# Order of work at six places in a one-core MLA and spatial-gating layer

## The chip, the cores and the metric

The kernel runs on one core of one Trainium2 chip. A core has five engines that run side by side: TensorE (PE in the profile; PEld are its weight loads), VectorE (DVE), ScalarE (ACT), GpSimd (POOL) and SyncE (SP), which here only issues DMAs. Each engine takes its instructions in the order in which the program gives them, and each instruction waits for the semaphores of what it needs. The metric is the device time of one execution in microseconds (us); lower is better.

## The reference

One decoder layer for 512 tokens of width 2048, all in float32. The input is normed and modulated by a conditioning vector c, and one wide projection gives all branches. Cut to what matters here:

```python
mod = c_act @ w_ada[l] + b_ada[l]
shift, scale, gate = jnp.split(mod, 3, axis=-1)
h = rmsnorm(x, attn_norm_g[l]) * (1.0 + scale[:, None]) + shift[:, None]
proj = h @ w_in[l]
q_lat, kv_lat, k_rope, z_mla, u, v, z_sgu, g_mla, g_sgu = split_cols(proj, IN_SPLITS)
q = (rmsnorm(q_lat, q_norm_g[l]) @ w_uq[l])...      # 16 heads, 128 plain and 64 rotary columns
kv = (rmsnorm(kv_lat, kv_norm_g[l]) @ w_ukv[l])...  # 16 heads, 128 key and 128 value columns
y_mla = causal_mla_attention(q_nope, q_rope, k_nope, k_rope, v_mla) * jax.nn.silu(z_mla)
y_sgu = chunked_causal_sgu(u, v, sgu_norm_g[l], w_spatial[l], b_spatial[l]) * jax.nn.silu(z_sgu)
merged = jax.nn.sigmoid(g_mla) * y_mla + jax.nn.sigmoid(g_sgu) * y_sgu
x = x + gate[:, None] * (merged @ w_out[l])
```

At the end stands a final norm. The spatial gate mixes v over the 128 tokens of a chunk with a lower triangular matrix for each of 16 groups.

## The kernel before

**Products in three matmuls.** To keep float32 accuracy, each operand is split in a high part (a cast to fp32r, on ACT) and a low part (the difference, on DVE), and a product is three matmuls: high by high, high by low, low by high. `mm3` (L147 to L150) issues them for ordinary products, L1384 to L1386 for the big projection. So each tile of weights that comes from DRAM costs an ACT cast and a DVE subtraction before TensorE can use it. The parts live in a few buffers that are used in turn (`w0h`/`w0l`, `w1h`/`w1l` and, in the projection, a third pair under the name X).

**The projection in blocks.** After the first products (L443 and the loops behind it) come 11 blocks of 28 granules. A granule is one slot of the order of work: 12 matmuls of 512 columns. The products of two column blocks are built from seven sums, so DVE also adds weights before it splits them (`v_sum`, `v_t3`), and POOL issues DMAs that add to what is in the buffer (`v_add`).

**The order inside a slot.** What happens beside the matmuls is entered by `on(slot, phase, f, ...)` (L703). In each slot the phases run in the order of L701, all but the last two ahead of the slot's matmuls, and inside a phase in the order of registration:

```python
FIRST, HIGH, EVAC, GATE, SPLIT, BACK, MISC, LOAD = range(8)
```

The cast of a granule's weights (`v_split`) stands in HIGH and its low part (`v_low`) in SPLIT, both two slots ahead of the granule's matmuls (two granules of a block have them in SPLIT and MISC). These are registered first, for all blocks at once (L741 to L765). Copies out of PSUM stand in EVAC, DMA issues in LOAD. All work of second rank stands in BACK: a small planner, `place` (L713), adds up DVE's cost by slot, moves an item on to the first slot with room, and enters it there in BACK.

**Work of second rank that the change touches.**
- *Shares* (L1008 to L1026, L1140): 52 partial sums of the shift vector with the columns of the first weights. Each share loads 256 KB by SP (`share_load`, LOAD phase, three buffers: `half0`, `half1`, `cosT`) and adds on DVE (`share`, BACK). The load of share i is entered in the slot in which share i-3 is done, and the first three loads all in one slot, three after the rotary tables' last step. Share i is placed at least four slots behind its load.
- *Mix* (L930 to L946, L971 to L996): for each of 16 groups `sgu_gain` scales v, `sgu_split` splits it (`sinT` high on ACT, `vl` low on DVE), and `sgu_mix`, in the next slot's MISC, is the three matmuls of the mixing product. `t_gate` (L952) is a gate product of 128x1024 on DVE that is placed in the same way.
- *Latent splits at the seam* (L1309, L1334 to L1348): in the last slots of the projection (-7 to -1) the ten tiles of the normed latents are split for the attention (`lat_split`, two ACT casts and two DVE subtractions for each pair), next to the three steps of the key's rotation (`key_rotary`, L1271) and the splits of the first attention weights (`ws.split_to`, L103). Slot 0 is where the attention's products begin: `rproj` (the rotary queries), `qproj`, `kproj`, `vproj`.

**The heads** (L1667 to L1719). For each head h: the scores, the softmax (masks, maxima and scaling on DVE, exponentials on ACT), in the meantime the next head's query product `qproj(h + 1)`, then ten 128x128 transposes of the probabilities in three groups (`transposes`, L1594), the next head's key product `kproj(h + 1)`, and the product with v. From head 12 on (`GATED`) the probabilities are scaled on DVE ahead of the transposes. Weights come through a stream (`Stream`, L68): `get` splits the weights of the next product ahead of their use and issues the DMAs of those behind. `bank()` gives the PSUM banks in turn; a bank is free when the copy of its last product out of it is done. The v product of a pair of heads is taken out of two banks by `finish` (L1538), which waits in the list `merging` until the next query product.

**Output gate dots** (L1434 to L1455, L54): the first half of the output gate needs 32 partial dots on DVE (`piece_sum`, 0.6 us each), spread over the heads by the table `PIECES`. The dots of an odd head stand inside its softmax, those of an even head behind its product with v; head 15's stand behind its transposes, right ahead of the sum that ends them.

Of the kernel before, what the change touches and what calls it, by code (L numbers as in the profile page):

```python
# [25 lines left out]
H = 16  # L26
# [24 lines left out]

SHIFT_AT = (17, 18, 19, 20, 20, 21, 22, 24, 25, 26, 27, 29, 31, 33, 35, 37)
NG = 8
PIECES = (2,) * 13 + (0, 3, 3)  # L54

INV_FREQ = np.array([
    0x3f800000, 0x3f3ff911, 0x3f0ff59a, 0x3ed7e89b, 0x3ea1e89b, 0x3e72d423, 0x3e361887, 0x3e088d77,
# [71 lines left out]
def trunk_layer(ctx, tc, xT, xn, c, vecs, pos, wada, w1, w2, wv, wv3, wv4, wh, wh15, wq, wqr, wk, wvv, wo, wsT, bsp, gfin, out,  # L129
# [53 lines left out]
    ws = Stream(nc, [(wp, f"wraw{i}") for i in range(3)], [(wp, f"w{i}") for i in range(2)])  # L183
# [83 lines left out]
    gq, gr, gk, gvv = {}, {}, {}, {}  # L267
# [45 lines left out]
    def get(i, ahead=1, run=1):  # L313
        r = ws.get(i, ahead)
        fs, pend[:] = pend[:run], pend[run:]
        for f in fs:
            f()
        return r
# [11 lines left out]
    def bank():  # L330
        n_bank[0] += 1
        return bank_at(ring[(n_bank[0] - 1) % len(ring)])
# [89 lines left out]
    for j in range(KC):  # L422
# [4 lines left out]
        wH, wL = get(g1[j], ahead=0)  # L427
# [76 lines left out]
    for j in range(KC):  # L504
        fix_begin(j)
        wH, wL = get(g2[j])
# [136 lines left out]
    for st in range(KC):  # L643
# [5 lines left out]
        wH, wL = get(gb[st], ahead=0 if st == KC - 1 else 1)  # L649
# [51 lines left out]
    FIRST, HIGH, EVAC, GATE, SPLIT, BACK, MISC, LOAD = range(8)  # L701

    def on(s, phase, f, *a):  # L703
        assert s >= done[0], (s, done)
        events.setdefault(s, {}).setdefault(phase, []).append(lambda: f(*a))
# [4 lines left out]
    def spend(s, us):  # L710
        busy[s] = busy.get(s, 0.0) + us

    def place(s, us, f, *a):  # L713

        def full(s):
            own, (a, b) = busy.get(s, 0.0) + us, (busy.get(s + d, 0.0) for d in (-1, 1))
            near = [sum(busy.get(s + d + k, 0.0) for k in range(5)) for d in range(-4, 1)]
            return own > 3.3 or own + max(a, b) > 5.75 or s < at_block[T0] + 22 and max(near) + us > 13.4

        while full(s):  # L720
            s += 1
        spend(s, us)
        on(s, BACK, f, *a)
        return s

    def run(s, *phases):
# [140 lines left out]
    for b in range(1, len(BLOCKS)):  # L867
# [11 lines left out]
        for key in (bl, br_, al, ar):  # L879
            if key[0] == "v":  # L880
                for t in range(2):
                    n, o = 2 * key[2] + t, key[1] * S
# [87 lines left out]
    for g in range(H):  # L970
        c, q = divmod(g, 4)  # L971
        on(s_, MISC, v_load, g)
        on(s_, LOAD, gain_load, g)
        a = s_ + 4
        on(a, BACK, sgu_scale)
        a = place(a, 0.29, sgu_weights)
        a = place(a, 0.29, sgu_weights_split)
        if g + 1 < H:
            on(a + 1, LOAD, sgu_load, g + 1)
        a = place(max(a, s_ + 5), 0.69, sgu_gain)  # L980
        a = place(a + 1, 0.69, sgu_split)
        s_ = max(a + 1, out_at[g - 2], max(ready["u", c, half] for half in range(2)) - 2)
        on(s_, MISC, sgu_mix, g)
        for half in range(2):
            out_at[g] = place(max(s_ + 1, ready["u", c, half] + 1), 0.46, sgu_out, g, half)
            last_out[g, half] = out_at[g]
        if q == 3:
            for half in range(2):
                stored[c, half] = max(last_out[k, half] for k in range(4 * c, g + 1)) + 1
                stored[c, half] = max(stored[c, half], gated[c, half] + 1)  # L990
                on(stored[c, half], LOAD, t_store, c, half)
# [141 lines left out]
    rope_end = rope_make(at_block[1] + 6)  # L1133
# [3 lines left out]
        on(s, MISC, shift_turn, 4 * q)  # L1137
        return place(s + 1, 0.6, shift_sum, 4 * q)

    used, biased = [rope_end + 3] * 3, []  # L1140
    s_ = used[0]
    for i, (q, ks, _) in enumerate(shares):
        on(used[-3], LOAD, share_load, i)
# [71 lines left out]
    for group in (((10, "lat8"), (11, "lat9")), ((12, "lat10"), ("plain", "sinT"))):  # L1215
# [9 lines left out]
        i = group[0][0]  # L1225
# [108 lines left out]
    on(s_att, LOAD, to_attention)  # L1334
    for i in range(10):
        on(s_att + (0, 0, 2, 2, 4, 4, 5, 5, 6, 6)[i], LOAD, lat_fetch, i)
        if i < 8:
            on((-7, -7, -5, -5, -3, -3, -2, -2)[i], BACK, lat_split, i)

    def first_weights(n):  # L1340
        ws.limit = gr[0] + n
# [2 lines left out]
    for n, s_ in enumerate((-7, -5, -3, -1)):  # L1344
        on(s_, LOAD, first_weights, n)
    on(-1, HIGH, lambda: ws.split_to(gr[0]))
    on(-1, MISC, lambda: ws.split_to(gq[0]))
    ws.next_raw, ws.next_part = 0, 1  # L1348

# [2 lines left out]
    for b in range(len(BLOCKS)):  # L1352
        if b == 1:
            ring[:], n_bank[0] = [5, 6], 0
        for g, (p, i) in enumerate(V7):
            s = done[0] = at_block[b] + g
            n = 1 if b or g else 2
# [15 lines left out]
            if i == 0 and p in (1, 5, 6):  # L1373
                which, banks = {1: ("y", y_of[b % 2]), 6: ("z", z_of), 5: ("w", z_of if b else (5, 6))}[p]
                v7[which] = [bank_at(k) for k in banks]
            ps = v7["y" if p < 5 else "z" if p > 5 else "w"]
            wH, wL = (w.rearrange("p (k h w) -> p k h w" if BLOCKS[b][0] == "v" else "p (h k w) -> p k h w", h=4, k=2)
                      for w in vparts.pop((b, g)))
# [20 lines left out]
    place = {}  # L1399
# [13 lines left out]

    krh, krl = at("krh", F32R), at("krl", F32R)
    hilo(krh, krl, kr[0])
    for i in (8, 9):
        lat_split(i)
    for key, at_ in ready.items():
        if at_ >= 0:
# [30 lines left out]
    def pieces_at(h):  # L1450
        k = sum(PIECES[:h])
        for i in range(k, k + PIECES[h]):
            piece_sum(i)
# [21 lines left out]
        load_before(gk[h], fetch, h)  # L1475


    qt, kt, vv, qs = {}, {}, {}, {}

    def qproj(h, meanwhile=None, then=None):  # L1480
        wH, wL = get(gq[h])
# [28 lines left out]
        tt(b[lo_], r[hi_], b[hi_].bitcast(F32), ALU.subtract)  # L1510
        qs[2 * p], qs[2 * p + 1] = a, b

    def kproj(h):
        wH, wL = get(gk[h])
        ps = bank()
        for k in range(4):
            sl = slice(k * P, (k + 1) * P)
            mm3(ps, wH[:, sl], wL[:, sl], lh[6 + k], ll[6 + k], k == 0, k == 3)
        return ps
# [28 lines left out]
    def scores(h):  # L1548
        qh, ql = qt.pop(h)
        kh, kl = kt.pop(h)  # L1550
        q2 = qs.pop(h)
        s3, s2, s1 = bank(), bank(), bank()
        dst = {3: s3, 2: s2[:, :384], 1: s1[:, :256], 0: s1[:, 256:384]}
        for i in (3, 2, 1, 0):
            ps = dst[i]
            n = (i + 1) * P
            q = slice(i * P, (i + 1) * P)
            mm3(ps, qh[:, q], ql[:, q], kh[:, :n], kl[:, :n], True, False)

            PE.matmul(ps, q2[:, q], krh[:, :n], start=False, stop=False)  # L1560
            PE.matmul(ps, q2[:, q], krl[:, :n], start=False, stop=True)  # L1561
        return dst
# [31 lines left out]
    def transposes(pr_, js):  # L1594
        w = sum((NB - j) * P for j in js)
        ps = bank()[:, :w]
        o = 0
        for j in js:
            for i in range(j, NB):
                PE.transpose(ps[:, o:o + P], pr_[i][:, j * P:(j + 1) * P], ident)  # L1600
                o += P
        th = at(f"th{js[0]}", F32R)[:, :w]
        tl = at(f"tl{js[0]}", F32R)[:, :w]
        parts = {}
        o = 0
        for j in js:
            n = (NB - j) * P
            parts[j] = (th[:, o:o + n], tl[:, o:o + n])
            o += n
        return parts, lambda: hilo(th, tl, ps)  # L1610
# [41 lines left out]
    ps = kproj(0)  # L1652
# [5 lines left out]
    def out_granule(cg, i, banks, ahead=1, run=1):  # L1658
        wH, wL = get(go[cg, i], ahead, run)
        for k in range(2):  # L1660
            j = 2 * i + k
            sl = slice(k * 512, (k + 1) * 512)
            for n in range(NB):
                tk = slice(n * P, (n + 1) * P)
                mm3(banks[n], mh[j][:, tk], ml[j][:, tk], wH[:, sl], wL[:, sl], j == 0, j == H - 1)

    for h in range(H):  # L1667
        if h == H - 1:
            ring[:], n_bank[0] = [4, 5, 6, 7], 0
            ws.split_to(go[0, 0])  # L1670
        dst = scores(h)
        more, odd = h + 1 < H, h % 2 == 1
        pair = h // 2 + 1
        first = go[0, 1] if not more else gr[pair] if not odd and 2 * pair < H else None
        pr_, shares_ = softmax(h, dst, (lambda: ws.split_to(first)) if first is not None else None)
        if more:
            qproj(h + 1, lambda: merge(1 if h == H - 2 else None))
            if not odd and 2 * pair < H:
                rps = rproj(pair)
        else:  # L1680
            pso = [bank_at(k) for k in range(NB)]
            for i in range(2):
                out_granule(0, i, pso)
        pa, fa = transposes(pr_, (0,))
        fa()
        if h < GATED:
            for n in range(NB):
                g_ = gt[h][:, n * P:(n + 1) * P]
                ACT.activation(g_, g_, AF.Copy, scale=shares_[:, n:n + 1])
        pb, fb = transposes(pr_, (1,))  # L1690
        fb()
        pc, fc = transposes(pr_, (2, 3))
        fc()
        if more:
            kps = kproj(h + 1)
            kfinish(h + 1, kps)
        else:
            merge()
            pieces_at(h)
            DVE.tensor_reduce(out=dots[:, 2 * KC:2 * KC + NG], in_=partial, axis=AX.X, op=ALU.add)  # L1700
            gate_sum(0, NG)
            out_granule(0, 2, pso)
            gate_turn(0, NG, bank(), nt(tp, [P, S], F32, "sig", bufs=3))()
        gate_ = gt[h]
        if h < GATED:
            gate_ = nt(tp, [P, S], F32, "sig", bufs=3)
            ACT.copy(gate_, turn(gt[h]))
        tps = turn(vt[h])
        ops = pv(h, {**pa, **pb, **pc})
        merge_a(h, ops, tps, gate_)  # L1710
        if not odd:
            pieces_at(h)
        if not odd and 2 * pair < H:
            m2 = at("m2", F32)
            swapped(m2, rps)
        if more and odd:
            rfinish(pair, rps, m2)
            vproj(pair)
# [192 lines left out]
```

## Time and profile before

| what | us |
|---|---|
| median of 3 runs (range) | 1564.72 (1563.97 to 1565.47) |
| the profiled execution | 1566.76 |
| its span, first to last instruction | 1565.1 |
| TensorE matmul busy | 1552.7 |
| VectorE busy | 1218.7 |
| ScalarE busy | 802.9 |
| GpSimd busy | 70.5 |

The profile is of one execution. A row of a timeline shows the start in us, the duration, the engine, the line of the kernel, the operation, the tiles (out<-in), the shape and the count; in brackets stands the idle time of the engine just before it and what ended it. Matmuls overlap, so the ends of their rows are modelled and a stall is read from the difference of two starts. A row of the chain of waits shows start, duration and name. A row of DMA issues shows the tiles, the queue, the count, the size and the us from issue to landing. `ps` are PSUM banks, `d` and `lat` are tiles of the latents' area that several things share, `hh`/`hl` high and low parts of the activations.

### The profile page before, as it was taken

The page shows a single profiled execution, that of the slowest core. Times are in us where ns is not written, and L with a number is a line of the kernel's source. Part 1 is how long each engine was busy: PE and PEld are TensorE (multiplying, and loading weights), DVE is VectorE, ACT ScalarE, POOL GpSimd, SP SyncE. Part 2 cuts the span into 40 slices and gives each one's busy share as a digit, 9 for nine tenths or more (in the row PEclk, how much of TensorE's full clock was granted, in tenths as well). Part 3 has the DMA queues.
Part 4 walks back from the last instruction along what each step waited for, and adds up shares of the span by engine and source line. Part 5 has one row for each costly group of instructions (what it writes and reads, how often), then busy time and mean ns, then how long its engine had stood idle before and what let it go on. Part 6 is the DMA issues. An engine that isn't in the chain of part 4 may idle for free.

```text
span 1565.1 us, 20574 instructions
## 1 busy us (share of the span) xinstructions
PE 1552.7 (99%) x7392; PEld 1296.2 (83%) x7392; DVE 1218.7 (78%) x1667; ACT 802.9 (51%) x1238; POOL 70.5 (5%) x67
## 2 busy tenths in 40 slices
PE   9999999999999999999999999999999999999998
PEld 7888778888888888888888888888888888888887
DVE  8989777778787879787879797878777777865753
ACT  4445555546545555545555565647655555532332
POOL 0000000101010101020100010100000000000000
PEclk9999999999999999999999999999999999999999
DMA  9979565858785877786867685967443433348722
GB/s 377 376 273 353 163 190 162 240 138 243 231 234 171 233 216 214 210 227 192 224 183 204 203 253 160 258 164 223 142 122 122 127 112 118 96 133 333 262 88 108
DMA packets 237224, 316.16 MB, mean 202 GB/s; under 512 B 16201, under 2 KB 184193, under 8 KB 231489
## 3 DMA queue, kind: packets, MB, share of 16 engines
q1 hardware_dynamic: 214210, 291.78, 57.0%
q0 software_dynamic: 22912, 23.07, 9.6%
q8 instruction: 58, 0.95, 0.2%
q14 instruction: 44, 0.36, 0.1%
HBM read 291.11 MB, written 23.68 MB: 201 GB/s over the span
## 4 chain that ended last, share of the span: by engine, by line
PE 91%; DMA 3%; DVE 3%; ACT 1%; issue 1%; SPq 0%; DVEq 0%; ACTq 0%
PE ps L1384 16%; PE ps L1386 16%; PE ps L1385 16%; PE ps L149 12%; PE ps L150 12%; PE ps L148 12%; PE ps L443 5%; DMA X<-in_wh 2%; PE ps L1600 1%; PE ps L1626 1%; DMA wraw<-in_w 1%; PE ps L1560 1%; PE ps L1561 1%; DVE X L136 1%; DVE d L136 0%
## 5 line engine op out<-in xcount | busy, mean ns | idle before, releaser
L136 DVE TENSOR_TENSOR X<-X,X 128x1024 fp32r<-128x1024 f32 (+2 forms) x111 | 130.5, 1182 | 32.7 <-ACT X L629 31.1
L629 ACT CAST X<-X 128x1024 fp32r<-128x1024 f32 x70 | 73.6, 1052 | 100.0 <-PE ps L1385 54.4
L629 ACT CAST w0h<-X 128x1024 fp32r<-128x1024 f32 x70 | 73.7, 1052 | 97.7 <-PE ps L1385 54.3
L629 ACT CAST w1h<-X 128x1024 fp32r<-128x1024 f32 x69 | 72.6, 1052 | 79.3 <-PE ps L1385 43.7
L136 DVE TENSOR_TENSOR w0l<-X,w0h 128x1024 fp32r<-128x1024 f32 x70 | 85.5, 1221 | 28.1 <-ACT w0h L629 27.9
L136 DVE TENSOR_TENSOR w1l<-X,w1h 128x1024 fp32r<-128x1024 f32 x69 | 84.3, 1221 | 24.7 <-ACT w1h L629 23.6
L119 DVE TENSOR_TENSOR w0l<-wraw,w0h 128x1024 fp32r<-128x1024 f32 (+4 forms) x61 | 64.3, 1053 | 40.4 <-ACT w0h L118 37.9
L118 ACT CAST w0h<-wraw 128x1024 fp32r<-128x1024 f32 (+4 forms) x61 | 56.0, 918 | 75.2 <-PE ps L150 21.1
L118 ACT CAST w1h<-wraw 128x1024 fp32r<-128x1024 f32 (+4 forms) x60 | 50.5, 841 | 83.7 <-PE ps L150 21.9
L136 DVE TENSOR_TENSOR X<-wraw,X 128x1024 f32<-128x1024 f32 (+1 forms) x65 | 79.3, 1221 | 17.2 <-ACT X L629 15.0
L1386 PE MATMUL ps<-w1l,hh 128*128 128x512 f32 x236 | 91.9, 390 | 0.2 <-DVE w1l L136 0.2
L1384 PE MATMUL ps<-w1h,hh 128*128 128x512 f32 x236 | 91.9, 389 | 0.0
L1385 PE MATMUL ps<-w1h,hl 128*128 128x512 f32 x236 | 91.9, 389 | 0.0
L1385 PE MATMUL ps<-w0h,hl 128*128 128x512 f32 x236 | 91.8, 389 | 0.0
L1384 PE MATMUL ps<-w0h,hh 128*128 128x512 f32 x236 | 91.8, 389 | 0.0
L1386 PE MATMUL ps<-w0l,hh 128*128 128x512 f32 x236 | 91.8, 389 | 0.0
L1386 PE MATMUL ps<-X,hh 128*128 128x512 f32 x232 | 90.6, 391 | 0.2 <-DVE X L136 0.2
L1384 PE MATMUL ps<-X,hh 128*128 128x512 f32 x232 | 90.4, 390 | 0.0
L1385 PE MATMUL ps<-X,hl 128*128 128x512 f32 x232 | 90.3, 389 | 0.0
L139 DVE SCALAR_TENSOR_TENSOR wada<-wada,cact 128x2048 f32<-128x2048 f32 x39 | 88.9, 2282 | 0.6 <-DMA wada<-in_wada 0.6
L119 DVE TENSOR_TENSOR w1l<-wraw,w1h 128x1024 fp32r<-128x1024 f32 (+4 forms) x60 | 57.4, 957 | 33.6 <-ACT w1h L118 32.7
L148 PE MATMUL ps<-hh,w1h 128*128 128x512 f32 x204 | 81.3, 399 | 0.0
(410 smaller groups left out, 4418.3 us busy)
## 6 DMA issues: line engine op xcount, KB each, us to landing
X<-in_wh SPq DMA_DIRECT2D x131, 512.0 KB, 5.0
wada<-in_wada SPq DMA_DIRECT2D x39, 1024.0 KB, 7.4
wraw<-in_wo SPq DMA_DIRECT2D x32, 512.0 KB, 4.2
wraw<-in_wh SPq DMA_DIRECT2D x21, 512.0 KB, 4.7
wraw<-in_wh POOLq DMA_DIRECT2D x21, 512.0 KB, 7.9
X<-in_wv SPq DMA_DIRECT2D x17, 512.0 KB, 3.7
X<-in_wh SPq DMA_DIRECT2D x22, 384.0 KB, 5.2
wraw<-in_w SPq DMA_DIRECT2D x16, 512.0 KB, 9.5
```

Of the source, the lines that this page charges most:

```text
L118: self.nc.scalar.copy(hi[:, :n], raw[:, :n])
L119: self.nc.vector.tensor_tensor(out=lo[:, :n], in0=raw[:, :n], in1=hi[:, :n].bitcast(F32), op=ALU.subtract)
L136: DVE.tensor_tensor(out=out, in0=in0, in1=in1, op=op)
L139: DVE.scalar_tensor_tensor(out=out, in0=in0, scalar=scalar, in1=in1, op0=op0, op1=op1, **kw)
L148: PE.matmul(ps, ah, bh, start=start, stop=False)
L149: PE.matmul(ps, ah, bl, start=False, stop=False)
L150: PE.matmul(ps, al, bh, start=False, stop=stop)
L443: PE.matmul(ps1[m], a[:, cols[m]], b, start=(j == 0 and a is wH and b is hh[j]), stop=False)
L629: ACT.copy(hi, t)
L1384: PE.matmul(ps[t].rearrange("p (h w) -> p h w", h=4), xh[:, tk], wH[:, k], start=st, stop=False, skip_group_check=True)
L1385: PE.matmul(ps[t].rearrange("p (h w) -> p h w", h=4), xl[:, tk], wH[:, k], start=False, stop=False, skip_group_check=True)
L1386: PE.matmul(ps[t].rearrange("p (h w) -> p h w", h=4), xh[:, tk], wL[:, k], start=False, stop=sp, skip_group_check=True)
```

## The change

It moves work at six places; nothing is computed in another way.

1. `PIECES`: head 12 gives up its two dots, heads 14 and 15 change from 3 and 3 to 2 and 4, head 15's four go ahead of its transposes, and two come last, where head 15's stood.
2. `sgu_split` is entered in the SPLIT phase in place of BACK, in the slot that the planner gives it as before.
3. The first three share loads are entered in three slots, one each, in place of one.
4. Of the latent splits, numbers 2 and 3 (slot -5) go from BACK to SPLIT.
5. Latent splits 6 and 7 go from slot -2, BACK, to slot -1, HIGH, behind the split of the first rotary query weights.
6. At head 14 the key product of head 15 is cut in two: its weights are split ahead of head 14's scores, its first half (six matmuls) runs ahead of head 14's transposes, the second half stays where the whole was. The PSUM bank of this product is so taken ahead of those of the transposes.

```diff
-PIECES = (2,) * 13 + (0, 3, 3)
+PIECES = (2,) * 12 + (0, 0, 2, 4, 2)
...
-    def place(s, us, f, *a):
+    def place(s, us, f, *a, phase=BACK):
...
-        on(s, BACK, f, *a)
+        on(s, phase, f, *a)
...
-        a = place(a + 1, 0.69, sgu_split)
+        a = place(a + 1, 0.69, sgu_split, phase=SPLIT)
...
-    used, biased = [rope_end + 3] * 3, []
+    used, biased = [rope_end + 3 + n for n in range(3)], []
...
-        if i < 8:
-            on((-7, -7, -5, -5, -3, -3, -2, -2)[i], BACK, lat_split, i)
+        if i < 6:
+            on((-7, -7, -5, -5, -3, -3)[i], SPLIT if i in (2, 3) else BACK, lat_split, i)
...
     on(-1, HIGH, lambda: ws.split_to(gr[0]))
+    for i in (6, 7):
+        on(-1, HIGH, lat_split, i)
...
-    def kproj(h):
-        wH, wL = get(gk[h])
-        ps = bank()
-        for k in range(4):
+    def kproj(h, ks=range(4)):
+        if ks[0] == 0:
+            kw[h] = (*get(gk[h], 1 if len(ks) == 4 else 0), bank())
+        else:
+            ws.split_to(gk[h] + 1)
+        wH, wL, ps = kw[h]
+        for k in ks:
...
+        if h == H - 2:
+            ws.split_to(gk[h + 1])
         dst = scores(h)
...
             for i in range(2):
                 out_granule(0, i, pso)
+            pieces_at(h)
+        halved = h == H - 2
+        if halved:
+            kproj(h + 1, range(2))
         pa, fa = transposes(pr_, (0,))
...
-            kps = kproj(h + 1)
+            kps = kproj(h + 1, range(2, 4) if halved else range(4))
...
             merge()
-            pieces_at(h)
+            pieces_at(H)
```

More of the change, by code (lines that the diff above doesn't have):

```diff
@@ L1415, in trunk_layer @@
     hilo(krh, krl, kr[0])
-    for i in (8, 9):
+    for i in range(8, 10):
         lat_split(i)
@@ L1475, in trunk_layer @@
         load_before(gk[h], fetch, h)
-    qt, kt, vv, qs = {}, {}, {}, {}
+    qt, kt, vv, qs, kw = {}, {}, {}, {}, {}
     def qproj(h, meanwhile=None, then=None):
```

## The prediction

> **What bounds the kernel now.** I read the page first, for the engine that sets the end, then the PE timeline for the places where it stands still, then for each such place the timeline of the engine that releases it, and the chain of waits for the one place that a transfer decides.
>
> ```profile
> span 1565.1 us, 20574 instructions
> PE 1552.7 (99%) x7392; PEld 1296.2 (83%) x7392; DVE 1218.7 (78%) x1667; ACT 802.9 (51%) x1238; POOL 70.5 (5%) x67
> ```
>
> TensorE is busy for 1552.7 of 1565.1 us, so an order of work can only win back short stalls. A stall is measured best from start to start. A 512-column matmul starts 0.23 us after the one ahead of it; what a step takes beyond that is lost. The edits speak to five groups of such steps. I take them one by one, and ask each time what is late next.
>
> **Share loads.** The stall is the step 394.11 to 394.90:
>
> ```profile
> 394.11 0.39 PE L1386 MATMUL ps<-w1l,s 128*128 128x512 f32 x1
> 394.90 0.50 PE L1384 MATMUL ps<-w0h,s 128*128 128x512 f32 x1 [0.40 <-ACT d L842]
> 395.24 0.39 PE L1385 MATMUL ps<-w0h,s 128*128 128x512 f32 x1
> ```
>
> 0.79 - 0.23 = 0.56 us, and the next step takes 0.34 instead of 0.23, another 0.11, which I add after every stall. Together 0.67. The chain of waits says why: a PSUM copy on ACT stands behind a cast that waits for one weight load.
>
> ```profile
> 381.37 11.85 DMA X<-in_wh
> 379.96 0.33 SPq L1014 DMA_DIRECT2D half<-in_w  x1
> 380.82 0.49 SPq L1014 DMA_DIRECT2D cosT<-in_w  x1
> 383.03 0.56 SPq L884 DMA_DIRECT2D v_d<-d  x1
> half<-in_w SPq DMA_DIRECT2D x1, 256.0 KB, 6.1
> v_d<-d SPq DMA_DIRECT2D x1, 256.0 KB, 12.4
> 389.07 0.75 DVE L139 SCALAR_TENSOR_TENSOR rx<-half,shift,rx 128x512 f32<-128x512 f32 x1
> 390.00 1.23 DVE L136 TENSOR_TENSOR w0l<-X,w0h 128x1024 fp32r<-128x1024 f32 x1 [0.18 <-ACT w0h L629]
> ```
>
> SP issues the three share loads (256 KB each, from 379.96), then this weight load (512 KB, at 381.37), then two stores of v. The edit leaves share 0 where it is and puts the weight load and both stores ahead of shares 1 and 2. Share 0 lands at 379.96 + 6.1 = 386.1 and the second store at 383.03 + 12.4 = 395.4. Between them land share 1, share 2, the weight load and two stores: 1536 KB in 9.3 us, 165 KB per us. If the queue keeps its order and its pace, the weight load now lands at 386.1 + 512/165 = 389.2, well ahead of its 393.2, and the 0.67 goes.
>
> What is late next: share 1, now behind 512 + 512 KB, lands at 386.1 + 1280/165 = 393.9. The planner still gives it its old slot, and DVE comes to it at 389.07. Behind it in DVE's order stands the w0l of row 390.00, which the third matmul of the group at 394.90 reads. Without a stall that matmul starts at 394.11 + 3 x 0.23 = 394.8. Now w0l ends 1.94 us after share 1 has landed (0.05, 0.75 less 0.09 overlap, 1.23), at 395.8: a new stall of 1.0 + 0.1. **Net +0.5.** Bounds: no stall if share 1 lands by 392.8 (net -0.7); landing last of the group, at 395.4, it costs 2.6 + 0.1 (net +2.0). I take the middle, since order and bytes are known and only the pace is assumed.
>
> The Trainium skill, page "DMA: Bandwidth & Descriptors", section "Rules for kernel authors", tells authors to issue a transfer early and wait for it late. By that rule moving share 1 back can only hurt; by the row of the 11.85 us it also frees the weight load, and my sum keeps both.
>
> **Mix's v split.** The edit moves the two halves of the split (ACT, then DVE) from the BACK phase of their slot to the SPLIT phase. There the low part of the weights was registered earlier and still comes first, so only what stands in BACK ahead of the split is passed. By the order of registration that is a gate product in 2 of the 16 slots, and nothing in the other 14.
>
> ```profile
> 777.01 1.22 DVE L136 TENSOR_TENSOR d<-d,d 128x1024 f32<-128x1024 f32 x1
> 778.14 0.68 DVE L136 TENSOR_TENSOR vl<-lat,sinT 128x512 fp32r<-128x512 f32 x1
> 778.27 0.39 PE L148 MATMUL ps<-sinT,whl 128*128 128x512 f32 x1
> 778.88 0.50 PE L149 MATMUL ps<-vl,whl 128*128 128x512 f32 x1 [0.22 <-DVE vl L136]
> 542.42 0.39 PE L148 MATMUL ps<-sinT,whl 128*128 128x512 f32 x1
> 542.73 0.50 PE L149 MATMUL ps<-vl,whl 128*128 128x512 f32 x1
> ```
>
> With vl ahead of the 1.22 us product it is ready 1.1 us earlier, more than the 0.61 - 0.23 = 0.38 that PE waits; at 542 the wait is 0.08. With 0.11 behind each: **-0.7**. The product is late by 0.6 instead, and only its store to DRAM waits for that. The other mix stalls of this stage stay. Bounds: -0.7 and 0.
>
> **Latent splits at the seam.** Here are two stalls, 1072.11 to 1072.66 and 1078.05 to 1078.67:
>
> ```profile
> 1065.63 2.51 ACT L1285 COPY d<-rx 32x512 f32<-32x512 f32 x4
> 1068.92 1.41 DVE L139 SCALAR_TENSOR_TENSOR hl<-b,vec,hh 128x512 fp32r<-128x512 f32 x2 [0.43 <-ACT hh L1313]
> 1071.39 1.22 DVE L136 TENSOR_TENSOR w1l<-wraw,w1h 128x1024 fp32r<-128x1024 f32 x1
> 1072.11 0.39 PE L1385 MATMUL ps<-w1h,hl 128*128 128x512 f32 x1
> 1072.66 0.50 PE L1386 MATMUL ps<-w1l,hh 128*128 128x512 f32 x1 [0.16 <-DVE w1l L136]
> 1077.80 0.83 ACT L118 CAST w0h<-wraw 128x768 fp32r<-128x768 f32 x1 [1.89 <-PE ps L1385]
> 1078.05 0.39 PE L149 MATMUL ps<-hl,w1h 128*128 128x512 f32 x1
> 1078.67 0.50 PE L150 MATMUL ps<-hh,w1l 128*128 128x512 f32 x1 [0.23 <-DVE w1l L119]
> 1088.09 1.22 DVE L119 TENSOR_TENSOR w0l<-wraw,w0h 128x1024 fp32r<-128x1024 f32 x1
> 1089.36 0.39 PE L149 MATMUL ps<-w0l,hh 128*128 128x256 f32 x1
> ```
>
> Splits 2 and 3 go ahead of the four copies of the key's rotation, so DVE no longer idles 0.43 for them. Its w1l ends 0.43 earlier and the first stall of 0.32 + 0.11 goes: **-0.4**. Splits 6 and 7 go behind the split of the first query weights, whose w1l then needs 1.4 us less of DVE ahead of it; ACT's two casts fit into its idle 1.89. So the second stall, 0.39 + 0.11, goes too. But it is **given back**: vproj's second matmul at 1089.36 starts as w0l ends (1088.09 + 1.22 = 1089.31), with no room. That w0l hangs on a run of ACT and DVE work that begins with the cast at 1077.80, which waits for the matmuls ahead of the second stall and not for those behind it. PE comes 0.5 earlier to a w0l that does not. I count 0 for it; the bounds are 0 and -0.5.
>
> **Output gate dots and the half key product.**
>
> ```profile
> 1341.66 0.68 DVE L139 SCALAR_TENSOR_TENSOR piece<-piece,cq 128x512 f32<-128x512 f32 x1
> 1347.25 0.39 PE L150 MATMUL ps<-hh,w0l 128*128 128x512 f32 x1
> 1348.21 0.44 PE L1600 MATMUL ps<-ident,hl 128*128 128x128 f32 x2 [0.58 <-DVE hl L143]
> 1349.28 0.47 PE L148 MATMUL ps<-hh,w1h 128*128 128x512 f32 x1
> 1366.85 0.68 DVE L119 TENSOR_TENSOR w0l<-wraw,w0h 128x512 fp32r<-128x512 f32 x1
> 1367.55 0.38 PE L1600 MATMUL ps<-ident,hl 128*128 128x128 f32 x2
> 1369.16 0.48 PE L148 MATMUL ps<-hh,w0h 128*128 128x512 f32 x1
> 1383.02 0.39 PE L148 MATMUL ps<-w0h,b 128*128 128x512 f32 x1
> 1383.33 0.50 PE L149 MATMUL ps<-w0l,b 128*128 128x512 f32 x1
> 1389.94 1.16 DVE L136 TENSOR_TENSOR hl<-ps,hh 128x512 fp32r<-128x512 f32 x2 [4.37 <-ACT hh L153]
> ```
>
> Head 13's transposes wait for its softmax: 0.96 - 0.23 = 0.73. Head 12's two dots (about 0.61 each) stand on DVE ahead of that softmax and leave: 1.2 against 0.73, **-0.73**. Head 14's ten transposes take 1369.16 - 1367.55 = 1.61 where head 13's take 1.07: **-0.54** is lost between them, on PSUM banks that the v product's split frees behind the w0l of 1366.85. The change moves that split ahead of the scores and puts six matmuls, 1.4 us, ahead of the transposes. The moved split may delay the softmax by up to its 0.68; the 1.4 covers it (without that cover it would cost the 0.68). The bank now taken first is one that was freed second, by a split that also comes 0.68 earlier. Head 14's third dot leaves, 0.6, which ends the 0.08 + 0.11 at 1383.33: **-0.2**. Four dots come into head 15's wait, 2.5 us inside the idle 4.37 of row 1389.94; without that cover they would delay the transposes' low parts, not the transposes. One load of output weights is issued later, still ahead of the whole first granule that comes before its use. Sum -1.5; bounds -1.5 and -0.7 (if the head 14 edits fail).
>
> **The sum.** -1.5 - 0.7 - 0.4 + 0.5 = -2.1 us. The profiled execution took 1566.76 (its span and 1.66 around it), so such a one would take 1564.7. The median of the runs is 1564.72, 2.0 lower; taking its stalls to be the same, it gives 1562.6.
>
> **The rivals.**
> (1) Share 1 lands in time. For: the idle of DVE ahead of 394 and a pace that differs between groups. Against: the same engines carry the same bytes. Time: -2.6 - 0.67 = -3.3, 1561.4. The Trainium skill, "DMA: Bandwidth & Descriptors", section "Anatomy of one DMA", has a fixed 2 us plus bytes over 436 GB/s, an estimated 2.6 us for 256 KB; by that share 1 would land long before 389 and this rival would hold. The trace's 6.1 us for share 0 speaks against it.
> (2) More is given back than at vproj. The head stalls come back where the next softmax step is as late; only 0.4 of the 1.5 and half of the mix stay: -0.3 - 0.4 - 0.4 + 0.5 = -0.6, 1564.1. Against: each released engine there waits for PE itself.
> (3) Slower: a late share holds SP too. The load of share 4 uses share 1's buffer, so SP cannot issue it, nor what stands behind it, until share 1 is done. If lateness passes from share 1 to 4, 7, 10 and on at 1.1 us each, the change turns slower with the second of these (-2.1 + 2 x 1.1 = 0.1), and five of them give +3.4, 1568.1. Against: the queue is backlogged there, so a later issue need not land later.
>
> **How the numbers follow.** Forecast 0.50, rival 1 0.22, rival 2 0.21, rival 3 0.07. A measurement of this kernel tells about 0.2%, 3.1 us, from no change. Faster by more than that is most of rival 1 and little else: 0.18. Slower is rival 3, less its milder half: 0.05. Within: 0.77. The range runs from all gains kept (-2.6 - 0.67 - 0.5 = -3.8, 1560.9) to share 1 landing last of its group (-0.6, 1564.1) with the scatter of the runs, 0.5: 1564.6.
>
> **What would show it.** Right: no long step at 394.1, but one on the third matmul behind it, with a DVE wait for a share's load; 778 and 542 in step; the seam's first stall gone and a new wait of about 0.5 at vproj's second matmul; even steps at heads 13 and 14. Wrong: a share wait that ends by 392.8, a mix that still waits for vl at 778, or scores that come late in head 14.

## The result and the profile after

| | before | after |
|---|---|---|
| median of 22 runs (range), us | 1565.48 (1563.97 to 1566.70) | 1563.18 (1562.49 to 1565.24) |
| ratio of the runs, 95% interval | | 0.9986 (0.9980 to 0.9992) |
| the profiled execution | 1566.76 | 1565.08 |

The change makes the kernel 2.2 us faster by the ratio, 2.3 by the medians. The forecast was a change of -2.1 and 1562.6. The interval excludes no change; the size, 0.14%, is below the 0.2% from which the forecast spoke of faster. The head of the page of the changed kernel:

```profile
span 1563.4 us, 20578 instructions
PE 1551.1 (99%) x7392; PEld 1297.3 (83%) x7392; DVE 1219.0 (78%) x1667; ACT 802.7 (51%) x1238; POOL 70.2 (4%) x67
```

The work of each engine is as before; only TensorE's waits differ. Now the places of the prediction, one by one, on the timelines of the changed kernel.

**Share loads.** TensorE first, then DVE:

```profile
394.08 0.39 PE L1387 MATMUL ps<-w0h,s 128*128 128x512 f32 x1
395.94 0.50 PE L1388 MATMUL ps<-w0l,s 128*128 128x512 f32 x1 [1.47 <-DVE w0l L136]
```

```profile
387.49 1.23 DVE L136 TENSOR_TENSOR w1l<-wraw,w1h 128x1024 fp32r<-128x1024 f32 x1 [0.77 <-ACT w1h L629]
394.00 0.75 DVE L139 SCALAR_TENSOR_TENSOR rx<-half,shift,rx 128x512 f32<-128x512 f32 x1 [5.28 <-DMA half<-in_w]
394.67 1.22 DVE L136 TENSOR_TENSOR w0l<-X,w0h 128x1024 fp32r<-128x1024 f32 x1
```

The old stall is gone and the foreseen new one is there: DVE stands 5.28 us at share 1, w0l waits behind it, and the third matmul of the group comes 1.86 - 0.23 = 1.63 us late. The landing at 394.0 is what the prediction had (393.9). The stall is larger than its 1.0, because TensorE was 0.5 us further on when it came there.

**A place not foreseen,** near 776:

```profile
776.02 0.39 PE L1387 MATMUL ps<-X,hl 128*128 128x512 f32 x1
776.83 0.50 PE L1388 MATMUL ps<-X,hh 128*128 128x512 f32 x1 [0.43 <-DVE X L136]
```

0.81 - 0.23 = 0.58 us are lost here for the low part of a product that no edit touches.

**Heads.** Head 13's transposes follow the product ahead of them after 0.23, where it was 0.96. Head 14's ten take 1369.08 - 1368.07 = 1.01, where it was 1.61:

```profile
1347.19 0.39 PE L150 MATMUL ps<-hh,w0l 128*128 128x512 f32 x1
1347.42 0.38 PE L1605 MATMUL ps<-ident,hl 128*128 128x128 f32 x2
...
1368.07 0.38 PE L1605 MATMUL ps<-ident,hl 128*128 128x128 f32 x2
...
1369.08 0.47 PE L148 MATMUL ps<-hh,w0h 128*128 128x512 f32 x1
```

These two traces leave a question. The waits at 395.94 and 776.83 cost 1.74 and 0.69 us with the 0.11 behind each, and yet the change is as fast as forecast with a smaller loss. And the profiled execution of before, 1566.76, was slower than all 22 timed runs (up to 1566.70). How many of the stalls on which the prediction rests belong to the kernel, and how many to the one execution that was profiled?

### The profile page after: what moved, and what is told of

The parts are those of the page before. It is cut to its first block, busy times and chain, and to the rows that moved or that the text cites. A ratio compares the mean times of both kernels' runs of the same rounds, so it can differ in the third digit from the quotient of the medians.

```text
span 1563.4 us, 20578 instructions
## 1 busy us (share of the span) xinstructions
PE 1551.1 (99%) x7392; PEld 1297.3 (83%) x7392; DVE 1219.0 (78%) x1667; ACT 802.7 (51%) x1238; POOL 70.2 (4%) x67
## 4 chain that ended last, share of the span: by engine, by line
PE 50%; DVE 1%; issue 0%; ACT 0%; DVEq 0%
PE ps L149 9%; PE ps L150 9%; PE ps L148 9%; PE ps L1388 6%; PE ps L1386 6%; PE ps L1387 6%; PE ps L1605 1%; PE ps L1631 1%; PE ps L1565 1%; PE ps L1566 1%; DVE d L136 0%; PE ps L1187 0%; PE ps L1177 0%; DVE X L136 0%; DVE w0l L119 0%
```

## The experiments

All times are medians in us (range); "before" is the kernel before, measured beside it on the same chip.

| kernel | runs | time | before | ratio (95%) |
|---|---|---|---|---|
| share loads alone | 11 | 1565.35 (1565.02 to 1566.17) | 1565.22 | 1.0000 (0.9991 to 1.0009) |
| share loads, share 1 a slot later | 11 | 1565.27 (1565.09 to 1565.58) | 1565.22 | 0.9999 (0.9991 to 1.0008) |
| mix alone | 11 | 1564.75 (1564.37 to 1565.07) | 1565.22 | 0.9995 (0.9987 to 1.0004) |
| heads alone | 11 | 1563.88 (1563.22 to 1564.78) | 1565.22 | 0.9991 (0.9982 to 0.9999) |
| before, again | 1 | 1565.13 | 1565.59 | |
| changed kernel, again | 1 | 1562.91 | 1565.59 | |
| seam alone | 11 | 1565.49 (1565.33 to 1566.37) | 1565.59 | 1.0000 (0.9991 to 1.0009) |
| seam and activations later | 11 | 1564.57 (1564.22 to 1565.33) | 1565.59 | 0.9994 (0.9985 to 1.0002) |
| dots' table alone | 11 | 1564.57 (1564.00 to 1564.78) | 1565.32 | 0.9994 (0.9985 to 1.0002) |
| all but the share loads | 11 | 1563.18 (1562.74 to 1565.02) | 1565.32 | 0.9987 (0.9979 to 0.9996) |
| the same, activations later | 11 | 1562.17 (1561.92 to 1563.34) | 1565.32 | 0.9981 (0.9972 to 0.9989) |
| all, share 1 and activations later | 11 | 1562.06 (1561.75 to 1562.45) | 1565.32 | 0.9979 (0.9970 to 0.9988) |

The intervals reach about 1.4 us to each side, so single edits are told apart by the traces. The experiments ran on three chips; the medians of before on them and in the first measurement (1565.48) lie within 0.4 us, which speaks against the chip as the reason for a long execution. All these kernels issue the same number of matmuls, so the start of matmul number k can be set side by side. The next table counts it from matmul 120 (at 18.6 us, behind the loads of the start), subtracts the second profile of before (below, "Both kernels once more"), and takes the difference from column to column; the headings give the stretch by the time of before. Negative is gained. The last column is the whole.

```
                        to 400  546    781    1093   1353   1372   end  | whole
before, first profile     1.01  0.05   0.14   0.35   0.05   0.01   0.04 |  1.65
changed, first profile    1.80 -0.21   0.23  -0.15  -0.71  -0.61  -0.18 |  0.17
changed, again            0.00 -0.21  -0.35  -0.11  -0.76  -0.61  -0.20 | -2.24
share loads alone         0.50  0.00   0.15  -0.16   0.06   0.02   0.05 |  0.62
share 1 a slot later      0.01  0.00   0.15  -0.02   0.03   0.02   0.03 |  0.22
mix alone                 0.01 -0.21  -0.41  -0.12   0.07   0.02   0.05 | -0.59
heads alone               0.00 -0.01   0.27  -0.12  -0.71  -0.61  -0.20 | -1.38
seam alone                0.31  0.01   0.11  -0.11   0.07   0.00   0.00 |  0.39
seam, activations later   0.04  0.18   0.45  -0.82  -0.12   0.03   0.05 | -0.19
dots' table alone         0.04  0.00   0.07  -0.09  -0.74   0.01  -0.21 | -0.92
all but share loads       0.01 -0.21  -0.17  -0.15  -0.71  -0.61  -0.18 | -2.02
same, activations later  -0.01 -0.22  -0.32  -0.76  -0.94  -0.62  -0.20 | -3.07
all, share 1, act. later  0.00 -0.22  -0.01  -0.80  -0.96  -0.60  -0.21 | -2.80
```

### The share loads alone, and with share 1 a slot later

The first kernel has this edit alone, the second this and the next:

```diff
-    used, biased = [rope_end + 3] * 3, []
+    used, biased = [rope_end + 3 + n for n in range(3)], []
```
```diff
-        s_ = place(max(used[-3] + 4, s_ + 1), 0.75 if len(ks) == 1 else 1.4, share, i)
+        s_ = place(max(used[-3] + (5 if i == 1 else 4), s_ + 1), 0.75 if len(ks) == 1 else 1.4, share, i)
```

> The kernel before with the share loads' edit alone. My working: the 0.67 us lost at 394.90 go, share 1 lands near 394 us, and the third matmul of its group starts when the low part w0l behind the share ends, at about 395.8; net +0.5 us against before. The trace of the changed kernel has this wait at 1.63 + 0.11 us (start 395.94), because TensorE reached the place about 0.5 us earlier there; if the start is set by the landing alone, it is again near 395.9 here, however early TensorE comes, and the net against before stays at +0.4 to +0.6. Rival 1 (share 1 lands in time): no step above 0.5 us there, -0.7. Rival 3 (lateness passes on to later shares): further DVE waits for share 4, 7, 10, more than +2. Also to be seen here: if a new wait near 776.8 us (0.59 in the changed kernel, not foreseen) appears in this kernel, it comes with the loads and not with the mix edit.

> The share loads' edit alone, and share 1 is allowed one slot later on DVE, so that the low part w0l stands ahead of it. Theory: the loss is only that DVE stands at share 1 with w0l queued behind; the loads' new order by itself is a gain. Then the steps at 394 to 396 are even, and the kernel is 0.67 us faster than before and 1.1 us faster than with the edit alone; DVE still idles for share 1 until about 394, with nothing urgent behind it. Rival: the wait moves to the next product (X low part) or to later shares, which now run a slot late through their buffers: between 0 and +0.5 against before.

Measured: 0.13 and 0.05 us slower in the medians, nothing within their intervals. The edit alone loses 0.50 by 400 us in its profile. Its timeline of TensorE, and that of DVE:

```profile
394.18 0.39 PE L1385 MATMUL ps<-w0h,s 128*128 128x512 f32 x1
394.71 0.50 PE L1386 MATMUL ps<-w0l,s 128*128 128x512 f32 x1
```

```profile
392.77 0.75 DVE L139 SCALAR_TENSOR_TENSOR rx<-half,shift,rx 128x512 f32<-128x512 f32 x1 [4.10 <-DMA half<-in_w]
393.44 1.22 DVE L136 TENSOR_TENSOR w0l<-X,w0h 128x1024 fp32r<-128x1024 f32 x1
```

The mechanism is that of the prediction (DVE idle at share 1, w0l behind it), but share 1 lands at 392.77, not 394.0, and the stall is 0.30. So my "start again near 395.9" fell: the landing moves from execution to execution. With share 1 a slot later the steps are even, as the theory said, but the 0.67 us that should then be won against before aren't there. The comparison was with a stall that the runs of before don't have: in the stretch to 400 this kernel and the second profile of before agree within 0.01.

### The mix alone, and the heads alone

The mix kernel passes `phase=SPLIT` in the one call for `sgu_split`; the heads' kernel has the table and the two halves of the key product, as in the change.

> The kernel before with the mix's v split in the SPLIT phase alone. My working: -0.7 us, the steps at 778.88 and 542.73 become even, all other steps stay. The changed kernel has a wait of 0.59 us at 776.83 for the low part of another product. If the mix edit makes it, it is here too, and the net is about -0.1. If it comes from where the weight load of 748 us landed (0.9 us later in that trace, ahead of any moved instruction), it is absent here, or present by chance only, and the net is -0.7.

> The kernel before with the output gate dots' table and the half key product alone. My working: -1.5 us: head 13's transposes no longer wait (0.73), head 14's ten transposes run through (0.54), the step at 1383.33 is even (0.2). Rival 2 (given back at the next softmax step): the same stalls gone but a new one behind them, -0.4 in all.

Measured: -0.47 and -1.34 in the medians. By the stretches the mix gains 0.21 at 542 and 0.41 up to 781; the heads 0.71 and 0.61 and 0.20. No wait is passed on behind them: the columns to their right are as in the kernels without these edits. Both leave the share loads alone, and in both profiles the stall of 394.90 is missing. That spoke for chance in the first profile, and the next two runs were for this.

### Both kernels once more

> The kernel before once more, unchanged, for a second profiled execution of it. In two kernels that leave the share loads as they were (the mix edit alone, the heads' edits alone) the step at 394.90 is 0.23 and not 0.79, that at 364.7 is 0.23 and not 0.36 and 0.34, and the first seam stall (1072.66) is gone without the seam edit. Theory: these stalls belong to the one execution that was profiled (1566.76, near the slowest of the runs), and not to the kernel; then they are absent here, the span is about 1563.8, and the two seam steps, the second at 1078.67 and vproj's at 1089.36, add up to about 0.75 again whatever their shares. Rival: they belong to the kernel, and the other kernels removed them by what they moved; then they are here again within 0.05 us, and the span is 1565.

> The changed kernel once more, unchanged, for a second profiled execution. Its first profile (1565.08, the third slowest of its 22 runs) has 1.63 us behind share 1 at 395.94 and 0.59 at 776.83. With the share loads' edit alone the wait at 395 was 0.30. Theory: both waits belong to the execution (to where two transfers landed); then the step at 395 is below 0.6, the one at 776 is even, and the span is about 1561.2. Rival: they belong to the kernel as a whole, and return within 0.2 us, with a span near 1563.

The theory held in both (the changed kernel's first profile is the second slowest of its runs, not the third). In before's second profile, TensorE at 394, at both seam places and at vproj:

```profile
393.83 0.39 PE L1386 MATMUL ps<-w1l,s 128*128 128x512 f32 x1
394.06 0.39 PE L1384 MATMUL ps<-w0h,s 128*128 128x512 f32 x1
...
1070.92 0.39 PE L1385 MATMUL ps<-w1h,hl 128*128 128x512 f32 x1
1071.19 0.50 PE L1386 MATMUL ps<-w1l,hh 128*128 128x512 f32 x1
...
1076.53 0.39 PE L149 MATMUL ps<-hl,w1h 128*128 128x512 f32 x1
1077.20 0.50 PE L150 MATMUL ps<-hh,w1l 128*128 128x512 f32 x1 [0.28 <-DVE w1l L119]
...
1087.76 0.28 PE L148 MATMUL ps<-w0h,hh 128*128 128x256 f32 x1
1087.87 0.36 PE L149 MATMUL ps<-w0l,hh 128*128 128x256 f32 x1
```

394.06 comes after 0.23, and the first seam step is 0.27 in place of 0.55. The second seam step and vproj's add up to 0.67 + 0.11 = 0.78 (0.75 in the first profile). In the changed kernel's second profile:

```profile
394.29 0.39 PE L1387 MATMUL ps<-w0h,s 128*128 128x512 f32 x1
394.52 0.39 PE L1388 MATMUL ps<-w0l,s 128*128 128x512 f32 x1
...
777.07 0.39 PE L148 MATMUL ps<-sinT,whl 128*128 128x512 f32 x1
777.30 0.39 PE L149 MATMUL ps<-vl,whl 128*128 128x512 f32 x1
...
1086.50 0.28 PE L148 MATMUL ps<-w0h,hh 128*128 128x256 f32 x1
1087.17 0.39 PE L149 MATMUL ps<-w0l,hh 128*128 128x256 f32 x1 [0.40 <-DVE w0l L119]
```

No stall at 394.52 and no more than 0.07 us near 776 (1.63 and 0.58 in the first profile), the mix step even, and the wait given back at vproj (0.67 where an unhindered 256-column step takes 0.12). The span is 1561.2 against 1563.4, so second profile against second profile gives -2.2, the measured change.

Why do the loads land earlier in the second profiles? SyncE's own waits between 371 and 383 us, in order: before, before again, changed, changed again.

```profile
SPq L1014 <- DMA rope_d<-half: 4.4, 1, 4.4
```
```profile
SPq L1014 <- DMA rope_d<-half: 3.5, 2, 3.3
```
```profile
SPq L1014 <- DMA rope_d<-half: 4.1, 1, 4.1
```
```profile
SPq L1014 <- DMA rope_d<-half: 3.0, 1, 3.0
```

(Line waited, total, times, longest.) The buffer of share 0 still holds a rotary table that is being stored to DRAM (`rope_d`), and SP holds share 0 and all that is queued behind it until that store has landed. In both first profiles the longest wait is 1.1 us longer than in the second. So a store decides when the group of the first shares can be issued; in before's first profile the stores themselves were also issued 0.8 us later (372.92 against 372.14). But a late issue alone makes no stall. The heads' kernel, with the loads in the old order, waited longer for the store than before's first profile and issued the weight load later (there 381.37):

```profile
SPq L1014 <- DMA rope_d<-half: 4.9, 1, 4.9
```
```profile
381.45 0.48 SPq L594 DMA_DIRECT2D X<-in_wh  x1
```
```profile
X<-in_wh SPq DMA_DIRECT2D x1, 512.0 KB, 10.1
```

This load took 10.1 us where before's took 11.85, so it landed at 391.6 and not at 393.2, and no matmul waited near 394. Over the nine profiles with the old order the load took 9.1 to 11.85 us and landed between 388.9 and 393.2; only the last of these landings made TensorE wait. So the stall of 394.90 came of a late issue and a slow transfer together, and why the transfer was slow in that execution stays open.

With the new order the issue tells more. Share 1 of the changed kernel, its issue on SP's timeline and its DMA row, in the first profile and in the second:

```profile
382.09 0.66 SPq L1014 DMA_DIRECT2D half<-in_w  x1
```
```profile
half<-in_w SPq DMA_DIRECT2D x1, 256.0 KB, 11.8
```
```profile
380.18 0.87 SPq L1014 DMA_DIRECT2D half<-in_w  x1
```
```profile
half<-in_w SPq DMA_DIRECT2D x1, 256.0 KB, 11.5
```

It takes 11.8 and 11.5 us from issue to landing; what differs by 1.9 us is the issue. 1.1 of these are SP's wait for the store, the rest lies in its other issues. The prediction's rival 1 cited the Trainium skill ("DMA: Bandwidth & Descriptors", section "Anatomy of one DMA") for an estimate of 2.6 us: the measured 11.5 is more than four times that, with a 512 KB load and two 256 KB stores ahead in the queue. The Trainium skill gives that formula for DMAs that GpSimd issues, and SyncE issued this one, so the estimate did not fit this transfer.

### The seam alone, and with the gate activations later

The first has the change's edits 4 and 5. The second also moves two activations (`squash`) into the list that runs behind the split of the first key weights:

```diff
-    for key, at_ in ready.items():
-        if at_ >= 0:
-            squash(key)
...
-    qproj(0, lambda: [f() for f in last_gates], lambda: ws.split_to(gvv[0]))
+    qproj(0, lambda: [squash(k_) for k_, a_ in ready.items() if a_ >= 0] + [f() for f in last_gates],
+          lambda: ws.split_to(gvv[0]))
```

> The kernel before with the latent splits' edits (2 and 3 to SPLIT, 6 and 7 to the last slot) alone. In the profiles without the edit the second seam step and vproj's step add up to 0.72 to 0.77, however the loss lies between them; with it, in the changed kernel, they are 0.23 and 0.67. Theory: vproj's low part w0l sets the time and the edit only moves the wait: no gain, 0.0 within 0.2 us of before, with vproj's second matmul waiting 0.4 to 0.5. Rival (my sum): -0.4 us, because the first stall at 1072.66 is the kernel's and ahead of the chain that vproj's w0l hangs on.

> The same, and the two gate activations on ACT (2.0 us and a table load of 1.28) that stand ahead of the cast of the first key weights are put behind it. The products on DVE that read them then end about 0.7 us earlier, and with them vproj's w0l, which stands behind them. Theory: that w0l is the only thing that holds the seam back: vproj's step is even, -0.5 to -0.6 us against the seam edit alone and against before. Rival: the wait moves on (to the key product's w1l, or to the rotary scores behind 1095), 0 gain.

Measured: the seam edit alone -0.10 in the median, 0.00 in effect: -0.11 in its column, and the kernels without the edit show -0.02 to -0.16 there as well. Its 0.31 in the first column is mostly the wait at 364.7 of before's first profile, here once more. Its vproj rows:

```profile
1087.47 0.28 PE L148 MATMUL ps<-w0h,hh 128*128 128x256 f32 x1
1088.15 0.39 PE L149 MATMUL ps<-w0l,hh 128*128 128x256 f32 x1 [0.40 <-DVE w0l L119]
```

With the activations later, ACT, DVE and vproj's rows of that kernel:

```profile
1080.65 0.62 ACT L118 CAST w1h<-wraw 128x512 fp32r<-128x512 f32 x1 [0.52 <-PE ps L149]
1081.29 1.28 ACT L857 ACT_TABLE_LOAD   x1
1082.59 2.01 ACT L857 ACTIVATE d<-d 128x1024 f32<-128x1024 f32 x2
```
```profile
1083.68 2.36 DVE L136 TENSOR_TENSOR d<-d,d 128x1024 f32<-128x1024 f32 x2 [1.68 <-ACT d L857]
1085.96 1.22 DVE L119 TENSOR_TENSOR w0l<-wraw,w0h 128x1024 fp32r<-128x1024 f32 x1
```
```profile
1087.48 0.28 PE L148 MATMUL ps<-w0h,hh 128*128 128x256 f32 x1
1087.59 0.28 PE L149 MATMUL ps<-w0l,hh 128*128 128x256 f32 x1
```

The cast no longer stands behind the activations, so DVE isn't kept by the low part of the key weights when the first activation is done, and w0l starts at 1085.96 where the kernel with the seam edit alone has 1086.88. vproj's step is 0.11 and the column gives -0.82, 0.71 more than the edit alone and more than the 0.5 to 0.6 expected, as the steps near 1094, behind vproj, also lose 0.22 less; the median is 1.0 us below before. So w0l behind the gate products was what held the seam with the edit in place. No run puts the activations later without the seam edit, so whether the edit is needed for this gain is not shown.

### The dots' table alone

The heads' kernel with `halved = False` and without the early split of the key weights.

> The kernel before with the output gate dots' table alone, without the half key product. My working: head 13's wait goes (-0.73) and the step at 1383.33 becomes even (-0.2), while head 14's ten transposes still take 1.61 us from first to key product: -0.9 us, and so -0.5 for the half key product in the kernel that has both (-1.3 measured). Rival: without the six matmuls in front, head 14's transposes start into a wait for the softmax, and the table alone gives 0.5 or less.

Measured -0.75 in the median, and by the stretches -0.74 (head 13), +0.01 (head 14), -0.21 (1383): the table has two of the three gains, the half key product the 0.61 of head 14. The half key product moves three things at once: the split of its weights, six matmuls, and the turn of its PSUM bank. Which of them makes head 14's transposes even is not shown.

### The change without the share loads, and two versions with the activations later

> The changed kernel with the share loads as before. My recorded term is +0.5 us for that edit, so this kernel would be 0.5 faster than the changed one, about -2.7 against before. Theory after the second profiles: in most executions neither order of the loads makes TensorE wait, the edit is worth 0.0 within 0.2 us, and this kernel stands at -2.2 against before like the changed one; the steps at 394 to 396 are even, or the first of them is late by up to 0.6.

> The changed kernel with the share loads as before and with the two gate activations behind the cast of the first key weights. If the seam gain of about 0.9 us (0.65 at vproj, 0.22 behind it) adds to the rest, -3.1 us against before, 1562.4, faster than both kernels. Rival: the gain is given back at the heads, -2.2.

> The changed kernel with share 1 one slot later on DVE (behind w0l) and with the two gate activations behind the cast. Same sum as the kernel with the loads as before, -3.1 us within 0.2: what this pair tells is whether any order of the loads is worth something in the median, and in the slowest of the runs. If a late share 1 makes the tail of the runs (two of 22 of the changed kernel lie 2 us above its median), this one has no run more than 1 us above its median.

Without the share edit the kernel takes 1563.18, the changed kernel's own median: the edit is worth nothing in the median, as the theory said, and the recorded +0.5 fell. Its slowest run, 1565.02, shows that executions 2 us above the median come without the edit too, so the tail isn't the edit's alone. The versions with the activations later take 1562.17 and 1562.06, -3.15 and -3.26 against before and 1.0 and 1.1 less than the kernel without the share edit, measured beside them, as the sum said. By the ratios both beat the changed kernel too (0.9981 and 0.9979 against 0.9986), but they were not measured beside it and the intervals overlap. With share 1 a slot later the slowest of 11 runs is 0.4 above the median; 11 runs are too few to call that a smaller tail.

The last one's profile lost time near 776 again:

```profile
774.52 0.39 PE L1387 MATMUL ps<-X,hl 128*128 128x512 f32 x1
775.09 0.50 PE L1388 MATMUL ps<-X,hh 128*128 128x512 f32 x1 [0.19 <-DVE X L136]
```

0.34 here, 0.27 in the kernel with the seam edit and the activations later, which has neither mix nor share edit, 0.58 in the changed kernel's first profile and none in its second. The low part that this matmul reads starts 2.2 us later in the changed kernel's first profile than in its second (775.56 against 773.36). 1.6 of the 2.2 are TensorE's own lag since the stall at 395.94 (398.36 against 396.79 for the same matmul). DVE lost the other 0.6 in front of one row, the w0l near 753; first profile, then second:

```profile
752.31 1.22 DVE L136 TENSOR_TENSOR wraw<-wraw,X 128x1024 f32<-128x1024 f32 x1
755.06 1.23 DVE L136 TENSOR_TENSOR w0l<-X,w0h 128x1024 fp32r<-128x1024 f32 x1 [1.54 <-ACT w0h L629]
```
```profile
750.76 1.22 DVE L136 TENSOR_TENSOR wraw<-wraw,X 128x1024 f32<-128x1024 f32 x1
752.85 1.23 DVE L136 TENSOR_TENSOR w0l<-X,w0h 128x1024 fp32r<-128x1024 f32 x1 [0.87 <-ACT w0h L629]
```

DVE waits there for ACT's cast, and in the first profile that cast waits for a weight load:

```profile
753.98 1.05 ACT L629 CAST w0h<-X 128x1024 fp32r<-128x1024 f32 x1 [3.60 <-DMA X<-in_wh]
```

All 14 profiles agree on this wait of DVE. It is 0.81 to 1.00 us in the ten in which the matmul near 776 starts at most 0.07 late, and 1.14, 1.20, 1.29 and 1.54 in the four in which it starts 0.18, 0.27, 0.34 and 0.58 late. In the last three of these the load ends the wait of ACT. So the loss near 776 goes with the execution and not with an edit. That a later landing makes it is read from these rows; no run moved that load.

## Why the prediction was right, and where it was wrong

The change of -2.1 stands against -2.2, and the time of 1562.6 against 1563.18. But the sum came out with two wrong terms that cancel: +0.5 for the shares and -0.4 for the seam, both 0 within what the runs tell. That the total fits to 0.1 is luck; the mechanism was right for the mix and the heads.

| step | forecast | second profiles | alone, by medians |
|---|---|---|---|
| share loads | +0.5 | 0.00 | +0.13 |
| mix's v split | -0.7 | -0.21 - 0.35 = -0.56 | -0.47 |
| seam | -0.4 | -0.11, as without the edit | -0.10 |
| heads | -1.5 | -0.76 - 0.61 - 0.20 = -1.57 | -1.34 |
| sum | -2.1 | -2.24 | -1.78 |

- **Share loads: the step that failed is "the 0.67 goes".** The stall at 394.90 stood in one profiled execution of before and in no other profile with the old order of loads (second profile, mix, heads, seam, seam with activations, dots' table, all but the shares, the same with the activations later: 0.23 in each). The runs showed 0 us there in place of the 0.67, and a stall of 0 to 1.63 behind share 1 in place of the 1.0. What is late next was foreseen rightly, by its place and its releaser. But the pace and the issue times of the sum were read from one late execution. The landing of 393.9 was that of the changed kernel's first profile (394.0), which is luck: in the other four profiles with the new order DVE starts on share 1 at 391.4 to 392.8, among them the edit alone (392.77, a stall of 0.30) and the changed kernel's second (391.77, none). Rival 1 (in time) held for the landing in the second profile and not for its gain. Rival 3 fell: no column behind 400 shows lateness handed on with this edit.
- **Mix: right,** both places and no other; by size 0.56 for 0.7, as the place near 776 takes or gives some tenths from one execution to the next.
- **Seam: the step that failed is "the first stall goes, -0.4".** In before's second profile that step is 0.27, not 0.55, so the edit had next to nothing to take away. That the second stall would be given back at vproj, counted at 0, was right: 0.55 us are lost there in the changed kernel, with the releaser w0l.
- **Heads: right,** term by term: 0.73, 0.54, 0.2 forecast; 0.76, 0.61, 0.20 found. Rival 2 fell: none of it is given back in a later column. Ten transposes take 1.01 us, a little less than the 1.07 of the forecast. The four dots at head 15 cost nothing that the columns show. That the banks were what head 14's transposes waited for was not tested by itself.
- **The absolute time** is 0.6 off: the three runs of before had a median of 1564.72, the 22 runs 1565.48, 0.8 higher, less the 0.1 to 0.2 that the change gave more. The sentence "taking its stalls to be the same" failed: the profiled execution was 2.0 us above that median, and 1.65 of them are in the first row of the table of stretches, 1.01 by 400 us (0.67 of it at 394.90) and 0.35 in the stretch with the seam: the places of the two terms that were wrong.

## What to carry to other kernels

Where the profiled execution is slower than the median by as much as the stalls under discussion, some of these stalls may be that execution's, as here: take a second profile of the same kernel ahead of the sum, and count only the waits that both show. Engine-to-engine waits with a fixed chain returned within 0.1 us in each profile that could have them (head 13's transposes, the mix step near 778, and the second seam step and vproj's step taken together); waits that a transfer's landing decides came and went by up to 1.6 us. Where a wait moves along a chain without a gain, as at the seam, look for the work that stands ahead of the last wait's releaser in its engine's order, and move that.

## What the runs showed of the hardware

The first share load was issued between 377.72 us (changed kernel, second profile) and 379.96 us (before, first), by when the store of the rotary table out of the buffer that it reuses had landed. The longest single wait of SyncE for it was 2.9 us (mix alone) to 4.9 us (heads alone). After the issue, share 1's load of 256 KB, with 1 MB issued between share 0 and it, took 10.6 to 11.8 us in the five profiles with the new order. The weight load of 512 KB behind the first three shares took 9.1 to 11.85 us in the nine profiles with the old order. What makes the store or these loads land early or late stays open.
